# FFN up-projection by seven block products instead of eight, with weight block sums on GpSimd and the residual kept in DRAM

## The chip, the cores and the metric

The kernel runs on one core of a Trainium2 chip. The metric is the device time of one launch in microseconds. Engines are named as the profile names them: PE (TensorE matmul), PEld (TensorE weight load), DVE (VectorE), ACT (ScalarE), POOL (GpSimd), SP (SyncE, which issues most transfers).

## The reference

Two layers of a diffusion backbone over 1280 tokens (256 context, 1024 latent), width 1024, all in fp32. After the token mixers each layer ends with a gated convolution FFN. This is the part that changes:

```
def _conv_ffn(h, w_up, conv_w, conv_b, w_down):
    u = jnp.einsum('bld,df->blf', h, w_up)
    ...
    u = sum(up[:, j:j + l] * conv_w[j] for j in range(CONV_W)) + conv_b
    a, g = jnp.split(u, 2, axis=-1)
    return jnp.einsum('blf,fd->bld', jax.nn.silu(a) * g, w_down)
...
        x = _layer_norm(ALPHA * x + g1_l * jnp.einsum('ble,ed->bld', m_l, w_out[i]), ln1_g[i], ln1_b[i])
        f_l = _conv_ffn(x * (1.0 + sc2_l) + sh2_l, ffn_up[i], ffn_conv_w[i], ffn_conv_b[i], ffn_down[i])
        x = _layer_norm(ALPHA * x + g2_l * f_l, ln2_g[i], ln2_b[i])
```

The hidden width is 2816, so `w_up` has 44 column tiles of 128: 22 value tiles and their 22 gate tiles. The convolution has three taps along the tokens.

## The kernel before

Activations lie transposed: a tile holds 128 features by a run of tokens. The precision of fp32 is had from three reduced-precision products: `split` (lines 211 to 213) writes a rounded high part by ACT (line 212) and the low rest by DVE (line 213), and every matmul is hi·hi + hi·lo + lo·hi. Weights are split as they arrive, activations once per stage.

Per layer the order is: input projection, linear and latent attention, output projection (`wout`), first norm (`ln`), FFN, second norm. The FFN runs over two parts of the tokens: 642 and 638 in layer 0 (context and latent, then latent), 512 and 512 in layer 1. For every one of the 22 hidden tiles `ffn_up` multiplies a value tile and a gate tile: each is 8 K tiles by 3 products by one or two token segments, in `dense` (line 323). ACT copies the result to a tile `u` (line 1141), then comes the convolution (ACT line 1146, DVE lines 1147 and 1148), the SiLU (line 1151), the gate product (line 1152) and the split of the hidden tile. Hidden tiles are multiplied down in groups of four or two (`groups`, line 61): `ffn_down` makes eight output tiles per group (matmuls of line 1180), and DVE adds each to the residual `y` in SBUF by one instruction from PSUM (line 1185).

A few things set the order of the work around it. `ffn_order` (line 43) issues the down product of a group after the first up tile of the next one. `wplan` lists all weights in the order of use, and `wahead` keeps up to four loads and three split weights ahead. Background work (`tick`) emits the norms, the modulation and layer 1's `ada` products a step at a time between the FFN steps. A scheduler then fixes one order for each engine, and every engine runs its list strictly in that order. Tiles of a kind share a fixed number of buffers (`u` 3, `t` 6, `h` 8, `hid` 16, `y` 8, split weights `w2` 7, loads `wst` 4); a new tile waits for the last reader of the one whose buffer it takes. All of PSUM is one tile `ps` of eight banks.

```
    def split(self, hi, lo, src):
        self.nc.scalar.copy(hi, src)
        self.nc.vector.tensor_tensor(lo, src, hi.bitcast(F32), op=ALU.subtract)
```

## Time and profile before

| what | value |
|---|---|
| time, median of 3 runs | 3468.95 us (3467.35 to 3469.02) |
| the profiled execution: span | 3473.9 us, mean granted TensorE clock 0.989 |
| PE busy | 3383.5 us (97%) |
| DVE busy | 2227.2 us (64%) |
| ACT busy | 1548.3 us (45%) |
| POOL busy | 398.5 us (11%) |
| DMA | mean 102 GB/s |

The profile gives one execution; its own time is the span, from the first to the last instruction, 4.95 us above the median of the runs. Busy time is the time in which an engine had at least one instruction in flight, so instructions that overlap count once. The FFN of layer 0 fills 950 to 1900 us of the span, that of layer 1 2705 to 3420 us.

### The profile page before, as it was taken

How to read it: one execution, taken by the hardware profiler on the slowest of the kernel's cores; microseconds unless marked ns; L12 is line 12 of the kernel's file. 1: busy time of each engine (PE TensorE's matmuls, PEld its weight loads, DVE VectorE, ACT ScalarE, POOL GpSimd, SP SyncE). 2: the span in 40 equal slices, each digit the busy share in tenths (PEclk: the TensorE clock that was granted, in tenths of full speed). 3: DMA queues.
4: the chain of work that ended last, by engine and by line, in shares of the span. 5: the costliest groups of instructions: out<-in, count | busy, mean ns of one | idle time of the engine just before them, and what ended most of it. 6: DMA issues, size and time to landing. Idle time of an engine off the chain costs nothing. (4 is left out here: it accounts for less than half of the span.)

```text
span 3473.9 us, 58101 instructions
## 1 busy us (share of the span) xinstructions
PE 3383.5 (97%) x23454; PEld 2919.4 (84%) x23454; DVE 2227.2 (64%) x3787; ACT 1548.3 (45%) x2867; POOL 398.5 (11%) x627
## 2 busy tenths in 40 slices
PE   8999999989999999999999999999999999999998
PEld 6997666768999999899999898766777888888897
DVE  3435878776774444675557734788877765687555
ACT  3334555544453333343334444555563544345433
POOL 0000333331010000000000000333310000001001
PEclk9999999989999999999999999999999999999999
DMA  8654111124223333432223444111124333323331
GB/s 291 203 185 135 29 55 41 40 83 141 74 73 116 122 116 132 147 104 78 75 73 120 161 135 136 36 42 51 38 96 131 96 92 97 97 91 116 98 92 49
DMA packets 174990, 354.95 MB, mean 102 GB/s; under 512 B 15552, under 2 KB 92160, under 8 KB 174720
## 3 DMA queue, kind: packets, MB, share of 16 engines
q1 hardware_dynamic: 174720, 351.23, 31.7%
q8 instruction: 184, 3.01, 0.4%
q14 instruction: 86, 0.70, 0.1%
HBM read 310.01 MB, written 36.44 MB: 100 GB/s over the span
## 5 line engine op out<-in xcount | busy, mean ns | idle before, releaser
L323 PE MATMUL ps<-h,w 128*128 128x320 f32 (+5 forms) x9600 | 1667.4, 334 | 15.1 <-ACT h L212 6.3
L323 PEld LDWEIGHTS ps<-h,w 128*128 128x128 f32 x9600 | 1532.0, 190 | 145.7 <-issue 7.0
L213 DVE TENSOR_TENSOR w<-ws,w 128x1024 fp32r<-128x1024 f32 x360 | 440.1, 1223 | 590.5 <-PE ps L323 294.5
L1180 PE MATMUL ps<-hid,w 128*128 128x256 f32 (+4 forms) x3696 | 576.6, 316 | 1.5 <-ACT hid L212 1.5
L1180 PEld LDWEIGHTS ps<-hid,w 128*128 128x128 f32 x3696 | 538.9, 189 | 36.1 <-issue 7.6
L212 ACT CAST w<-ws 128x1024 fp32r<-128x1024 f32 x360 | 378.8, 1053 | 416.6 <-PE ps L1180 291.2
L919 PE MATMUL ps<-h,h 96*128 96x512 f32 (+1 forms) x1200 | 325.4, 392 | 18.7 <-DVE w L947 14.4
L919 PEld LDWEIGHTS ps<-h,h 96*128 96x128 f32 x1200 | 200.0, 194 | 78.1 <-issue 21.1
L1147 DVE SCALAR_TENSOR_TENSOR t<-u,vec,t 128x642 f32<-128x642 f32 (+3 forms) x176 | 144.6, 821 | 181.9 <-ACT t L1146 181.8
L932 ACT ACTIVATE w<-ps,sm 128x768 f32<-128x768 f32 (+2 forms) x272 | 208.9, 774 | 113.0 <-DVE sm L928 91.2
L1141 ACT COPY u<-ps 128x512 f32<-128x512 f32 (+4 forms) x264 | 118.2, 483 | 310.7 <-PE ps L323 310.7
L1185 DVE SCALAR_TENSOR_TENSOR y<-ps,mod,y 128x320 f32<-128x320 f32 (+5 forms) x376 | 197.0, 557 | 69.0 <-PE ps L1180 68.3
L945 PE MATMUL ps<-ident,w 128*128 128x128 f32 x1312 | 222.3, 287 | 12.1 <-ACT w L932 12.0
L945 PEld LDWEIGHTS ps<-ident,w 128*128 128x128 f32 x1312 | 152.0, 144 | 70.6 <-issue 35.5
L965 POOL TENSOR_SCALAR dg<-ident,sm 128x128 f32<-128x128 f32 x144 | 99.8, 697 | 954.7 <-DVE sm L963 833.4
L1137 POOL MEMSET u<- 128x1 f32 (+1 forms) x264 | 20.9, 102 | 1616.9 <-DVE t L1148 1462.4
L969 PE MATMUL ps<-w,hid 128*64 128x128 f32 x2624 | 196.8, 282 | 3.8 <-DVE y L979 2.0
L969 PEld LDWEIGHTS ps<-w,hid 128*64 128x64 f32 x2624 | 151.8, 139 | 41.2 <-issue 29.1
L921 DVE TENSOR_REDUCE sm<-ps 128x1 f32<-128x1024 f32 x128 | 156.3, 1221 | 43.8 <-PE ps L919 38.8
L949 ACT COPY w<-ps 128x256 f32<-128x256 f32 (+1 forms) x272 | 128.2, 474 | 94.0 <-PE ps L945 92.0
L716 POOL TENSOR_TENSOR hid<-hid,hid 128x512 f32<-128x512 f32 x108 | 146.3, 1371 | 98.5 <-ACT hid L696 69.0
L1146 ACT ACTIVATE t<-u,vec 128x642 f32<-128x642 f32 (+3 forms) x176 | 153.8, 874 | 0.4
(195 smaller groups left out, 3279.4 us busy)
## 6 DMA issues: line engine op xcount, KB each, us to landing
ws<-in_up_dram SPq DMA_DIRECT2D x176, 512.0 KB, 3.6
ws<-in_down_dram SPq DMA_DIRECT2D x88, 512.0 KB, 3.5
ws<-in_ada_dram SPq DMA_DIRECT2D x80, 512.0 KB, 4.8
ws<-in_w_in_dram SPq DMA_DIRECT2D x48, 512.0 KB, 4.3
ws<-in_w_out_dram SPq DMA_DIRECT2D x32, 512.0 KB, 3.7
y<-in_ada_dram SPq DMA_DIRECT2D x16, 512.0 KB, 8.3
ws<-in_w_v_dram SPq DMA_DIRECT2D x16, 512.0 KB, 4.0
hid<-in_xT_dram SPq DMA_DIRECT2D x16, 320.0 KB, 6.1
```

What stands on the lines that cost most here:

```text
L212: self.nc.scalar.copy(hi, src)
L213: self.nc.vector.tensor_tensor(lo, src, hi.bitcast(F32), op=ALU.subtract)
L323: nc.tensor.matmul(ps[:, i, 0:n], w_[:, k, :], h[k][:, part, o:o + n], start=(k == 0 and q == 0), stop=(k == 7 and q == 2))
L716: nc.gpsimd.tensor_tensor(X[n][:], blk(E[n][:, 0, cs[i]]), qx[:], op=ALU.mult)
L919: nc.tensor.matmul(sc[:, o:o + n], q[qa][0:96, qs], K[ka][0:96, o:o + n], start=(x == 0), stop=(x == 2))
L921: nc.vector.tensor_reduce(st[:, 1:2], sc[:, 0:1024], axis=AX.X, op=ALU.max)
L932: nc.scalar.activation(P[:, c0:c1], sc[:, c0:c1], AF.Exp, bias=st[:, 2:3], scale=MSCALE, accum_out=st[:, 3 + j:4 + j])
L945: nc.tensor.transpose(ps[:, t_], P[:, 128 * (t0 + t_):128 * (t0 + t_) + 128], self.ident[:])
L969: nc.tensor.matmul(op[64 * i:64 * i + 64, 0], V[h // 2][t_ // 5][:, t_ % 5, r:r + 64], pts[i][:, t_], start=(t_ == 0), stop=(t_ == nk - 1) ...
L1146: nc.scalar.activation(v[:, 0:n], u[:, 1:1 + n], AF.Identity, scale=cw(j, 1), bias=self.vec[l][:, V_CB + j:V_CB + j + 1])
L1180: nc.tensor.matmul(pb[i][:, 0:n], w[w_][:, x, ms], p.hh[f0 + x][hp][:, o - 1:o - 1 + n], start=(x == 0 and q == 0), stop=(x == gn - 1 and ...
L1185: nc.vector.scalar_tensor_tensor(t, pb[i][:, o:o + n], self.md(l, 5, m, who), t, op0=ALU.mult, op1=ALU.add)
```

## The change

The up product of a pair (value tile A, gate tile G) is written as a 2 by 2 block product. The rows of blocks are the tiles A and G, the inner blocks are the two halves of K (four K tiles each), and the columns are the left and the right half of the part's tokens. Eight half-size products become seven, by the Strassen scheme in Winograd's form:

- For every pair POOL makes four weight sums of 128x512 (`wload`): x0 = G_lo + G_hi, x1 = x0 - A_lo, z0 = A_lo - G_lo, z1 = A_hi - x1. The seven weight blocks (A_lo, A_hi, G_hi and the four sums) are each split by ACT and DVE, as 128x512.
- Once per part `sums` makes the seven activation blocks: DVE forms 16 sums of half the tokens, and 28 half-width blocks are split. It takes the place of `hsplit` (8 full-width splits).
- `ffn_up` issues seven products of 4 K tiles by 3, that is 84 matmuls of 322, 318 or 256 columns, where there were 96 (layer 0: 256 and 386, or 320 and 318 columns) or 48 (layer 1: 512 columns). They go into three banks of a ring of four, in the order 0, 5, 6, 1, 4, 3, 2. In place of ACT's copies, ACT makes two half-width copies (`s1` and one quarter of the result) and DVE five half-width adds from PSUM (`s6`, `s7` and three quarters). Products 1, 4, 3 and 2 accumulate on banks that ACT or DVE has read before.
- The residual is no longer in SBUF during the FFN. The first norm stores its result to a DRAM tile `yd` (SP), the modulation overwrites `y` in place, and of every output tile of the down product ACT scales the PSUM result into a tile `t`, and a transfer that POOL issues adds it to `yd` in DRAM. Before the second norm its tokens are loaded back (SP). The very last group alone still adds by DVE, to rows loaded ahead.
- The groups are one and seven times three hidden tiles for every part. The parts of layer 0 are 644 and 636 tokens. Loads go up to eight list entries ahead, splits up to six buffers.

The diff, cut to its core (the removed comments and unchanged pieces left out):

```diff
-    for n in [2] + [4] * 5 if (l, part) == (NL - 1, 1) else [4] * 4 + [2] * 3:
+    for n in [1] + [3] * 7:
         out.append((f, n))
         f += n
     return out
 
+UNIT = {1: 1024, 3: 256}
...
+PAIR = (0, 5, 6, 1, 4, 3, 2)
...
+PARTS = ((0, 644), (644, T)), ((CTX, 768), (768, T))
...
+        if self.ffn:
+            return self.ps[:, 4:6, :]
...
-                    q += [(a["up"][l, j], [128, 8, 128]) for j in (x, NF + x)]
+                    q += [((l, part, x), i) for i in PAIR]
                 else:
                     f0, gn = groups(l, part)[x]
-                    w, u = a["down"][l, f0:f0 + gn].rearrange("f p o -> p f o"), 1024 // gn
-                    q += [(w[:, :, u * i:u * i + u], [128, gn, u]) for i in range(gn)]
+                    w, u = a["down"][l, f0:f0 + gn].rearrange("f p o -> p f o"), UNIT[gn]
+                    q += [(w[:, :, u * i:u * i + u], [128, gn, u]) for i in range(1024 // u)]
...
+        elif shape == PAIR[0]:
+            l, _, f = src
+            A, G = self.ws([128, 8, 128]), self.ws([128, 8, 128])
+            nc.sync.dma_start(A[:], self.a["up"][l, f])
+            nc.sync.dma_start(G[:], self.a["up"][l, NF + f])
+            x, z = self.yk(shape=(128, 2, 4, 128)), self.yk(shape=(128, 2, 4, 128))
+            lo, hi = slice(0, 4), slice(4, 8)
+            for out, p, q, op in ((x[:, 0], G[:, lo], G[:, hi], ALU.add), (x[:, 1], x[:, 0], A[:, lo], ALU.subtract),
+                                  (z[:, 0], A[:, lo], G[:, lo], ALU.subtract), (z[:, 1], A[:, hi], x[:, 1], ALU.subtract)):
+                nc.gpsimd.tensor_tensor(out, p, q, op=op)
+            self.wsum[src] = {0: (A, A[:, lo]), 1: (A, A[:, hi]), 2: (z, z[:, 1]), 3: (G, G[:, hi]), 4: (x, x[:, 0]), 5: (x, x[:, 1]), 6: (z, z[:, 0])}
...
+        while self.wl < min(self.wi + 8, self.wlim):
+            if self.wsp < self.wl - 3 and isinstance(self.wq[self.wl][0], tuple) and self.wq[self.wl][1] == PAIR[0] and len(self.wsum) > 1:
+                break
+            self.wload(self.wl)
             self.wl += 1
-        while self.wsp < min(self.wi + 3 - len(self.begun), self.wl):
-            shape = self.wq[self.wsp][1]
-            hi, lo = self.w2(shape, F32R), self.w2(shape, F32R)
-            self.split(hi[:], lo[:], self.wst.pop(self.wsp)[:])
-            self.wrd[self.wsp] = (hi, lo)
-            self.wsp += 1
+        n = 2 * len(self.begun)
+        i = self.wi
+        while i < min(self.wl, self.wlim):
+            src, shape = self.wq[i]
+            n += 1 if isinstance(src, tuple) else 2
+            if n > 6:
+                break
+            if i == self.wsp:
+                if isinstance(src, tuple):
+                    t = self.w2([128, 2, 4, 128], F32R)
+                    self.split(t[:, 0], t[:, 1], self.wsum[src].pop(shape)[1])
+                    if not self.wsum[src]:
+                        del self.wsum[src]
+                    self.wrd[i] = (t[:, 0], t[:, 1])
+                else:
+                    hi, lo = self.w2(shape, F32R), self.w2(shape, F32R)
+                    self.split(hi[:], lo[:], self.wst.pop(i)[:])
+                    self.wrd[i] = (hi, lo)
+                self.wsp += 1
+            i += 1
...
+    def ytiles(self, W):
+        t = [self.yk(shape=(128, 2, W)) for _ in range(4)]
+        return [t[k // 2][:, k % 2, :] for k in range(8)]
...
-        Y = [t[:, c0:c1] for t in y]
+        if load is not None:
+            Y = self.ytiles(W)
+            for k in range(8):
+                nc.sync.dma_start(Y[k], load[:, k, c0:c1])
+            yield
...
+    def sums(self, F, W):
+
+        nc, n = self.nc, W // 2
+        left, right = slice(0, n), slice(n, W)
+        X = [[None] * 4 for _ in range(7)]
+        for i in (0, 1):
+            for k in range(4):
+                X[i][k] = self.hid([128, 2, n], F32R)
+                self.split(X[i][k][:, 0], X[i][k][:, 1], F[4 * i + k][:, left])
+        free = []
+        for k in range(4):
+            T_ = {}
+            if k > 1:
+                t = self.yk(F32R, (128, 2, 2, n))
+                T_ = {3: t[:, 0], 2: t[:, 1]}
+            for i in (4, 5, 6) if k > 1 else (4, 5, 3, 6, 2):
+                if not free:
+                    t = self.hs([128, 2, 2, n])
+                    free = [t[:, 0], t[:, 1]]
+                T_[i] = free.pop(0)
+            t, t2 = self.tt([128, 2, n]), self.tt([128, 2, n])
+            z = {4: t[:, 0], 5: t[:, 1], 3: t2[:, 0], 6: t2[:, 1]}
+            b11, b12, b21, b22 = F[k][:, left], F[k][:, right], F[4 + k][:, left], F[4 + k][:, right]
+            nc.vector.tensor_tensor(z[4], b12, b11, op=ALU.subtract)
+            nc.vector.tensor_tensor(z[5], b22, z[4], op=ALU.subtract)
+            nc.vector.tensor_tensor(z[3], b21, z[5], op=ALU.subtract)
+            nc.vector.tensor_tensor(z[6], b22, b12, op=ALU.subtract)
+            for i in (5, 6, 4, 3):
+                self.split(T_[i][:, 0], T_[i][:, 1], z[i])
+            self.split(T_[2][:, 0], T_[2][:, 1], b22)
+            del t, t2, z
+            for i, t in T_.items():
+                X[i][k] = t
+        return X
...
+        def product(i, bank, first):
+            hi, lw = self.wnext()
+            for k in range(4):
+                for q, (w_, part) in enumerate(((hi, 0), (hi, 1), (lw, 0))):
+                    nc.tensor.matmul(bank[:, 0:w], w_[:, k, :], X[i][k][:, part, :], start=(first and k == 0 and q == 0),
+                                     stop=(k == 3 and q == 2), skip_group_check=True)
+        def bank():
+            self.ring = (self.ring + 1) % 4
+            return self.ps[:, self.ring, :]
...
+        st = self.tt([128, 2, w])
+        s1, s6 = st[:, 0], st[:, 1]
+        b1 = bank()
+        product(0, b1, True)
+        nc.scalar.copy(s1, b1[:, 0:w])
+        b2 = bank()
+        product(5, b2, True)
+        nc.vector.tensor_tensor(s6, b2[:, 0:w], s1, op=ALU.add)
+        b3 = bank()
+        product(6, b3, True)
+        s7 = self.tt([128, w])
+        nc.vector.tensor_tensor(s7[:], b3[:, 0:w], s1, op=ALU.add)
+        product(1, b1, False)
+        for c, d, at in pieces(0):
+            nc.scalar.copy(U[0][:, at:at + d - c], b1[:, c:d])
+        product(4, b2, False)
+        plus(U[1], 1, b2, s7)
+        product(3, b3, False)
+        plus(U[1], 0, b3, s6)
+        product(2, b2, False)
+        plus(U[0], 1, b2, s1)
...
-                for i, o, n, cd, who in p.outs:
-                    if i in ss:
-                        t = y[m][:, cd:cd + n]
-                        nc.vector.scalar_tensor_tensor(t, pb[i][:, o:o + n], self.md(l, 5, m, who), t, op0=ALU.mult, op1=ALU.add)
+                if last:
+                    for i, o, n, cd, who in p.outs:
+                        if i in ss:
+                            t = p.Y[m][:, cd - base:cd - base + n]
+                            nc.vector.scalar_tensor_tensor(t, pb[i][:, o:o + n], self.md(l, 5, m, who), t, op0=ALU.mult, op1=ALU.add)
+                else:
+                    t, e = self.tt([128, 644]), 0
+                    for i, o, n, cd, who in p.outs:
+                        nc.scalar.activation(t[:, cd - base:cd - base + n], pb[i][:, o:o + n], AF.Identity, scale=self.md(l, 5, m, who))
+                        e = cd - base + n
+                    nc.gpsimd.dma_start(yd[:, m, base:base + e], t[:, 0:e], accum_op=ALU.add)
...
-        h = net.hsplit(Ff[0], P[0].c1 - P[0].c0)
+        net.ffn = True
+        X = net.sums(Ff[0], P[0].c1 - P[0].c0)
+        Ff[0] = y[0] = None
...
+                    X = net.sums(Ff[1], p.c1 - p.c0)
+                    Ff[1] = y[1] = None
...
+                    else:
+                        d0, d1 = p.done
+                        p.Y = net.ytiles(d1 - d0)
+                        for k in range(8):
+                            nc.sync.dma_start(p.Y[k], yd[:, k, d0:d1])
```

The first place is DVE's list in layer 1's second part, where the group's up tile runs (`w` split weights, `u` the up result, `t` work tiles, `hid` the hidden tile, `hal` the two carried columns). Before, in a row:

```order
L213 TENSOR_TENSOR w_29839<-ws_29798,w_29838 128x1024
L1147 SCALAR_TENSOR_TENSOR t_29832<-u_29828,vec_76,t_29832 128x514
L1148 SCALAR_TENSOR_TENSOR t_29832<-u_29828,vec_76,t_29832 128x514
L1139 COPY u_30180<-hal 128x2
L213 TENSOR_TENSOR w_29883<-ws_29836,w_29882 128x1024
L1147 SCALAR_TENSOR_TENSOR t_29870<-u_29866,vec_76,t_29870 128x514
L1185 SCALAR_TENSOR_TENSOR y_25169<-ps,mod_78,y_25169 128x258
L1148 SCALAR_TENSOR_TENSOR t_29870<-u_29866,vec_76,t_29870 128x514
L1185 SCALAR_TENSOR_TENSOR y_25169<-ps,mod_78,y_25169 128x255
L1152 TENSOR_TENSOR t_29870<-t_29832,t_29870 128x514
```

And now (L256 is the split, L1260 and L1264 are `s6` and `s7`, L1251 the three result quarters, `y` the tiles with the weight sums):

```order
L1260 TENSOR_TENSOR t_31511<-ps,t_31511 128x256
L256 TENSOR_TENSOR w_31574<-ws_31512,w_31573 128x1024
L1264 TENSOR_TENSOR t_31571<-ps,t_31511 128x256
L256 TENSOR_TENSOR w_31590<-ws_31533,w_31590 128x512
L256 TENSOR_TENSOR w_31606<-y_31537,w_31606 128x512
L1251 TENSOR_TENSOR u_31507<-ps,t_31571 128x256
L256 TENSOR_TENSOR w_31622<-y_31538,w_31622 128x512
L1251 TENSOR_TENSOR u_31507<-ps,t_31511 128x256
L256 TENSOR_TENSOR w_31664<-ws_31533,w_31664 128x512
L1282 SCALAR_TENSOR_TENSOR t_31638<-u_31507,vec_76,t_31638 128x514
L1251 TENSOR_TENSOR u_31505<-ps,t_31511 128x256
L1283 SCALAR_TENSOR_TENSOR t_31638<-u_31507,vec_76,t_31638 128x514
```

The adds to the residual are gone, and between the reads of the product banks stand splits of weights for later products.

The second place is POOL's list at a down product of the same part. Before, POOL only clears the edge columns of `u`:

```order
L1137 MEMSET u_30142 128x2
L1137 MEMSET u_30180 128x2
L1137 MEMSET u_30224 128x2
L1137 MEMSET u_30262 128x2
L1137 MEMSET u_30306 128x2
```

Now the weight sums (L218) and the accumulating transfers (L1330, to the DRAM tile) share the list:

```order
L1225 MEMSET u_33235 128x2
L1330 DMA y_26302<-t_32962 128x513
L1330 DMA y_26302<-t_32984 128x513
L218 TENSOR_TENSOR y_33099<-ws_33096 128x512
L1330 DMA y_26302<-t_33012 128x513
L218 TENSOR_TENSOR y_33099<-y_33099,ws_33095 128x512
L218 TENSOR_TENSOR y_33100<-ws_33095,ws_33096 128x512
L218 TENSOR_TENSOR y_33100<-ws_33095,y_33099 128x512
L1330 DMA y_26302<-t_33034 128x513
```

The sums of a coming pair stand behind transfers that wait for ACT's scaled output.

The third place is PE's list where layer 0 goes from its first to its second part. Before, layer 1's `ada` products (L263) stand between the last up tile of one and the first of the other, which walks the K tiles `h` one by one:

```order
L323 MATMUL ps<-h_9261,w_13555 128x386
L263 MATMUL ps<-ws_13748,st 32x256 x4
L263 MATMUL ps<-ws_13754,st 32x256 x4
L323 MATMUL ps<-h_13760,w_13616 128x320
L323 MATMUL ps<-h_13760,w_13616 128x318
```

Now (`h` and `hid` of numbers above 14000 are blocks of the new part, L1318 the down product):

```order
L306 MATMUL ps<-ws_14264,st 32x256 x4
L1242 MATMUL ps<-h_14294,w_14174 128x318 x3
L1242 MATMUL ps<-h_14295,w_14191 128x318 x3
L1242 MATMUL ps<-hid_14270,w_14157 128x318 x3
L1242 MATMUL ps<-hid_14273,w_14157 128x318 x3
L1242 MATMUL ps<-hid_14276,w_14157 128x318 x3
L1242 MATMUL ps<-hid_14279,w_14157 128x318 x3
L1318 MATMUL ps<-hid_13715,w_14429 128x256
L1318 MATMUL ps<-hid_13715,w_14429 128x388
```

The first matmuls of the new part need blocks that `sums` makes on DVE and ACT; six matmuls of the waiting down product stand there before the pair goes on, the other 138 behind it.

## Rows read from the trace of the kernel before

**Rows 1.** The page's part 1, busy time of each engine.
```profile
PE 3383.5 (97%) x23454; PEld 2919.4 (84%) x23454; DVE 2227.2 (64%) x3787; ACT 1548.3 (45%) x2867; POOL 398.5 (11%) x627
```

**Rows 2.** Busy time in windows: layer 0's FFN parts, then layer 1's (columns first).
```profile
core 0: us, PE busy (x) PEld busy (x) DVE busy (x) ACT busy (x) POOL busy (x), PEclk, DMA share, GB/s
950.00:1420.00 470.00, 469.06 (x3321) 450.60 (x3320) 262.73 (x382) 174.49 (x257) 14.54 (x87) 1.00 0.35 115
1420.00:1900.00 480.00, 479.24 (x3285) 474.26 (x3284) 290.93 (x424) 190.48 (x278) 9.15 (x47) 1.00 0.31 95
2705.00:3060.00 355.00, 355.00 (x1533) 287.65 (x1532) 229.29 (x325) 160.06 (x215) 12.72 (x88) 1.00 0.32 94
3060.00:3420.00 360.00, 359.55 (x1968) 310.66 (x1967) 239.51 (x372) 163.53 (x220) 12.18 (x46) 1.00 0.31 97
```

**Rows 3.** The same view, stretches with matmuls of one width: 319, 512, 257.
```profile
1700.00:1800.00 100.00, 100.00 (x683) 100.00 (x682) 50.44 (x71) 32.30 (x46) 0.88 (x8) 1.00 0.26 78
2800.00:2900.00 100.00, 100.00 (x434) 81.20 (x433) 59.27 (x83) 42.95 (x58) 1.78 (x28) 1.00 0.31 95
3230.00:3250.00 20.00, 20.00 (x169) 20.00 (x168) 12.16 (x22) 4.08 (x5) 0.10 (x1) 1.00 0.36 107
```

**Rows 4.** Groups of DVE and ACT: operands, shapes, count | busy us, mean ns | idle before.
```profile
L213 DVE TENSOR_TENSOR w<-ws,w 128x1024 fp32r<-128x1024 f32 x360 | 440.1, 1223 | 590.5 <-PE ps L323 294.5
...
L213 DVE TENSOR_TENSOR h<-hid,h 128x512 fp32r<-128x512 f32 x32 | 20.6, 686 | 0.0
...
L904 DVE TENSOR_TENSOR h<-ps,h 64x256 fp32r<-64x256 f32 x24 | 9.9, 411 | 0.8 <-ACT h L903 0.7
...
L1185 DVE SCALAR_TENSOR_TENSOR y<-ps,mod,y 128x320 f32<-128x320 f32 (+5 forms) x376 | 197.0, 557 | 69.0 <-PE ps L1180 68.3
...
L1147 DVE SCALAR_TENSOR_TENSOR t<-u,vec,t 128x642 f32<-128x642 f32 (+3 forms) x176 | 144.6, 821 | 181.9 <-ACT t L1146 181.8
```

**Rows 5.** DVE's instructions in time during attention: start us, us, instruction.
```profile
358.80 0.76 DVE L693 TENSOR_TENSOR hid<-u 128x512 f32<-128x512 f32 x1
359.49 0.41 DVE L703 TENSOR_TENSOR hid<-hid,u 128x256 f32<-128x256 f32 x1
359.82 0.41 DVE L924 TENSOR_REDUCE sm<-ps 128x1 f32<-128x256 f32 x1
...
360.75 0.90 DVE L703 TENSOR_TENSOR hid<-hid,u 128x256 f32<-128x256 f32 x1
...
362.75 1.50 DVE L765 SCALAR_TENSOR_TENSOR hid<-u 128x256 f32<-128x256 f32 x1
```

**Rows 6.** POOL's instructions in the same stretch.
```profile
360.09 1.28 POOL L716 TENSOR_TENSOR hid<-hid,hid 128x512 f32<-128x512 f32 x1 [1.08 <-ACT hid L696]
361.32 1.23 POOL L712 TENSOR_TENSOR hid<-u,hm 128x512 f32<-128x512 f32 x1
362.63 2.76 POOL L716 TENSOR_TENSOR hid<-hid,hid 128x512 f32<-128x512 f32 x2
```

**Rows 7.** Line L716: duration ns min/median/max, first and last start, form.
```profile
L716 POOL TENSOR_TENSOR hid<-hid,hid x108: 1262/1286/1773, 348.4 to 2505.4; 128x512 f32<-128x512 f32 x108
```

**Rows 8.** DVE's instructions in time at the start of layer 0's FFN.
```profile
935.52 1.23 DVE L213 TENSOR_TENSOR w<-ws,w 128x1024 fp32r<-128x1024 f32 x1 [4.08 <-issue]
936.66 1.00 DVE L1055 SCALAR_TENSOR_TENSOR y<-ps,mod,y 128x320 f32<-128x320 f32 x2
937.58 5.04 DVE L213 TENSOR_TENSOR h<-hid,h 128x642 fp32r<-128x642 f32 x6
...
944.59 1.55 DVE L213 TENSOR_TENSOR h<-hid,h 128x642 fp32r<-128x642 f32 x2
```

**Rows 9.** The page's parts 3 and 6: a DMA queue; two issues, us to landing.
```profile
q1 hardware_dynamic: 174720, 351.23, 31.7%
...
ws<-in_down_dram SPq DMA_DIRECT2D x88, 512.0 KB, 3.5
...
y<-in_ada_dram SPq DMA_DIRECT2D x16, 512.0 KB, 8.3
```

More of the change, by code (lines that the diff above doesn't have):

```diff
@@ L86, in __init__ @@
         self.pairs = 2
+        self.ffn, self.ring = False, 0
         self.begun = []
@@ new lines, in wload @@
+    def wload(self, i):
+        nc, (src, shape) = self.nc, self.wq[i]
+        if not isinstance(src, tuple):
+            t = self.ws(shape)
+            nc.sync.dma_start(t[:], src)
+            self.wst[i] = t
+        elif shape == PAIR[0]:
[9 more added lines that the diff above has]
+            self.wsum[src] = {0: (A, A[:, lo]), 1: (A, A[:, hi]), 2: (z, z[:, 1]), 3: (G, G[:, hi]), 4: (x, x[:, 0]), 5: (x, x[:, 1]), 6: (z, z[:, 0])}
@@ L1102, in ffn_part @@
         p = Bag()
-        c0, c1 = (((0, 642), (642, T)), ((CTX, 768), (768, T)))[l][part]
+        c0, c1 = PARTS[l][part]
         W = c1 - c0
@@ L1117, in ffn_part @@
         else:
-            p.segs = halves(W) if W > 512 else [(0, W)]
-            p.place = [2 + o for o, _ in p.segs]
+            p.segs, p.place = [(0, W)], [2]
             p.npos, p.zero = W + 2, [(W + 2, W + 4)]
@@ L1126, in ffn_part, with ffn_up @@
         return p
-    def ffn_up(self, l, p, f, h):
+    def sums(self, F, W):
[31 more added lines that the diff above has]
+        return X
+    def ffn_up(self, l, p, f, X):
         nc = self.nc
         cw = lambda j, i: self.vec[l][:, V_CW + 3 * j + i:V_CW + 3 * j + i + 1]
-        vs, n = [], p.npos
-        for j in (f, NF + f):
-            ps = self.sc2()
-            self.dense(ps, p.segs, self.wnext(), h)
+        n, W = p.npos, p.c1 - p.c0
+        w = W // 2
+        U = []
+        for _ in range(2):
             u = self.u([128, 646])
@@ L1137, in ffn_up, with pieces, plus @@
                 nc.gpsimd.memset(u[:, z0:z1], 0.0)
+            U.append(u)
+        for u, j in zip(U, (f, NF + f)):
             if p.part:
                 nc.vector.tensor_copy(u[:, 0:2], self.hal[:, j, :])
-            for i, (o, w) in enumerate(p.segs):
-                nc.scalar.copy(u[:, p.place[i]:p.place[i] + w], ps[:, i, 0:w])
+        def pieces(half):
+            for (o, m), at in zip(p.segs, p.place):
+                c, d = max(o, w * half), min(o + m, w * half + w)
+                if c < d:
+                    yield c - w * half, d - w * half, at + c - o
+        def product(i, bank, first):
[7 more added lines that the diff above has]
+            return self.ps[:, self.ring, :]
+        def plus(u, half, b, t):
+            for c, d, at in pieces(half):
+                nc.vector.tensor_tensor(u[:, at:at + d - c], b[:, c:d], t[:, c:d], op=ALU.add)
+        st = self.tt([128, 2, w])
[19 more added lines that the diff above has]
+        plus(U[0], 1, b2, s1)
+        vs = {}
+        for x in (1, 0):
+            u, j = U[x], (f, NF + f)[x]
             if not p.part:
@@ L1189, in ffn_down, with ln_last @@
                 _, _, n, cd, _ = p.outs[ss[0]]
-                yield from self.ln_last(l, cd, cd + n, y)
-    def ln_last(self, l, c0, c1, y):
+                yield from self.ln_last(l, cd, cd + n, [t[:, cd - base:cd - base + n] for t in p.Y])
+    def ln_last(self, l, c0, c1, Y):
         nc = self.nc
         W = c1 - c0
-        Y = [t[:, c0:c1] for t in y]
-        ps, p2 = self.sc2(), self.sc2()
+        ps, p2 = self.ps[:, 0:2, :], self.ps[:, 2:4, :]
         for k in range(8):
@@ L1343 @@
         store = [(net.xs, 0), (out, CTX)][l]
-        ln2 = [net.ln(l, *p.done, y, V_LN2G, V_LN2B, store) for p in P]
+        ln2 = [net.ln(l, *p.done, None, V_LN2G, V_LN2B, store, load=yd) for p in P]
         for op, part, x in ffn_order(l):
@@ L1357 @@
                     net.tick()
-                for _ in net.ffn_down(l, p, x, y):
+                for _ in net.ffn_down(l, p, x, yd):
                     net.tick(1, but=ada)
@@ L1361 @@
                     net.bg.insert(0, ln2[0])
-                if part and x == len(groups(l, part)) - 2 and l == 0:
-                    net.drain(ln2[0])
-                    nx = net.modulate(1, 0, 0, 640, net.loader(net.xs, 0, 640), F)
-                    for _ in nx:
-                        pass
+                if part and x == len(groups(l, part)) - 2:
+                    if l == 0:
+                        net.drain(ln2[0])
+                        nx = net.modulate(1, 0, 0, 640, net.loader(net.xs, 0, 640), F)
+                        for _ in nx:
+                            pass
+                    else:
[3 more added lines that the diff above has]
+                            nc.sync.dma_start(p.Y[k], yd[:, k, d0:d1])
+        del X
+        net.ffn = False
         if l == 0:
```

77 lines of the change are left out of this document (38 added, 39 removed).

## The prediction

> **What bounds the kernel now.** I read the engines' busy time first. PE is busy for 97% of the span, DVE for 64%, ACT for 45%, POOL for 11% [rows 1]. A kernel like that gets shorter by what PE is spared, until another engine's list becomes longer than PE's. So the second view is the windows of the two FFN stretches, the only ones that change [rows 2]. There PE is at 99 to 100% and its clock is granted in full (1.00, so 2.4 GHz). DVE works 553.7 of 950 us in layer 0 (58%) and 468.8 of 715 us in layer 1 (66%), ACT 365.0 and 323.6 us, POOL almost nothing, and the DMA share is about 0.32. The third view, stretches with matmuls of one width, gives PE's price per matmul: 683 in 100 us are 146.4 ns each at about 319 columns, 434 are 230.4 ns at 512, and 169 in 20 us are 118.3 ns at about 257 [rows 3]. A matmul of half the columns therefore costs 0.51 of a whole one. In the last stretch PEld is busy all the time: every narrow matmul has a weight load of its own, and it stays covered.
>
> **What PE is spared.** Layer 0: a pair had 96 matmuls and has 84. 12 x 146.4 ns x 44 pairs are 77 us; the new ones have 322 or 318 columns, a little more than the old mean, which gives back 2: **75 us**. Layer 1: 48 x 230.4 ns = 11.06 us per pair become 84 x 118.3 ns = 9.94 us, 1.12 us x 44 pairs = **49 us**. The eighth product saved is worth half as much there, because halves are dearer per column. Together -124 us: PE's FFN work would be 875 and 666 us. The order of PE's list has exactly 44 x 2 x 84 up matmuls, so the saving itself is certain; the question is what the others need in this time.
>
> **What DVE gets.** Back to back, its instructions start sooner than the one before ends: 0.41 us instructions stand 0.33 us apart [rows 5], so I take 0.08 us off each mean.
> - Weight splits: seven of 512 columns (0.686, so 0.606) for two of 1024 (1.223, so 1.143) [rows 4]: +1.96 us per pair, +86 us per layer.
> - Five adds from PSUM per pair: 0.411 us at 256 columns [rows 4], so 0.33 each, 1.65 per pair in layer 1 (+73 us). For 322 columns I go on along the line through 0.411 (256) and 0.686 (512): 0.48, so 0.40 each (+88 us).
> - The residual adds go: 0.557 [rows 4], so 0.48 us, x 224 in layer 0 (-107 us) and x 136 in layer 1 (-65 us).
> - `sums` adds 16 half-width subtractions and costs 28 half-width splits for 8 whole ones: about +12 us for the second part.
>
> Layer 0: 553.7 + 86 + 88 - 107 + 12 = **633 us**. Layer 1: 468.8 + 86 + 73 - 65 + 10 = **573 us**. Against 875 and 666 both still fit. ACT gets seven half-size copies for two, two narrow copies and the scaling, and loses the whole-width copies; it stays near 60 to 66%, beside PE. The transfers that add to DRAM read and write some 75 MB more, about as many bytes again as a quarter of the traffic now; at 0.32 that is no bound. Reloading the residual and storing it on SP's queue I cost at nothing: each has at least one whole pair (15 us) before its reader, against landings of 3.5 to 8.3 us [rows 9]; without that cover it would be one landing per norm, 8 us.
>
> **What POOL gets, and what it does to DVE.** 176 sums per layer of 128x512. The same form in attention takes 1.286 us [rows 7], so **227 us** per layer; POOL has room. But what POOL does is not free for DVE. In attention [rows 5, 6] a 256-column DVE instruction with both inputs in SBUF that takes 0.41 us alone takes 0.90 when it starts inside a POOL instruction (360.75, under POOL's 360.09 to 361.37), and 1.50 in the next (362.75), while the reduction that reads PSUM is untouched. So POOL's instruction blocks DVE's two-input ones. How much of 227 us falls on DVE is not in this trace; the ends are 0 (POOL runs only beside ACT waits and PSUM reads) and all of it. I take the share of time in which DVE would have such an instruction in hand, since that is what a sum meets. In layer 1, a pair of 15.1 us holds 7 weight splits x 0.606, 4/3 splits for the down product of about 0.87, 4 convolution taps of 0.67 and 2 more of 0.61: 9.3 us, 0.61; with the norms 0.65. In layer 0 the same list over 19.9 us, with the norms, is 0.55.
>
> The Trainium skill, "SBUF — State Buffer", section "Who interferes with whom", states this as a rule: DVE and GpSimd have one pair of ports in common, an instruction holds it whole, and the other fully blocks when a DVE instruction has two SBUF inputs and the GpSimd one reads SBUF. The rows agree with it (0.41 to 0.90 us), and taken at full price for each sum it speaks against this change: it would give the 3529 us of the first rival below instead of my 3440.
>
> DVE then needs 573 + 0.65 x 227 = 721 us in layer 1, against 666 on PE: DVE-bound, so **+55 us**. Layer 0: 633 + 0.55 x 227 = 758 of 875 us (87%). That fits as a sum but not at every moment: product 2 writes the bank that DVE must have read after product 4, with product 3 alone (12 matmuls, 1.8 us) as cover, and between those reads stand weight splits that a sum may block. I charge 0.45 us per pair, **+20 us**, between 0 and 1 us.
>
> **Starts of a part.** At the FFN's start DVE was idle for 4 us and had 8 splits [rows 8]; now it has some 36 half-width instructions more than PE's first product covers: +5 us for each layer, **+10**. At layer 0's second part the first matmuls of the new part stand ahead of most of a down product, and the blocks take buffers that the last products read: **+10 us** (0 to 20). Layer 1's is within DVE's sum already.
>
> Transfers that POOL issues I cannot price from this trace: the ends are 0 and the 8.3 us landing [rows 9] for each. `t` has six buffers, one output comes every 2.1 to 2.65 us (18 matmuls at 118.3 or 146.4 ns), so a landing has 12 us of cover; I take 0.
>
> **Sum.** -124 + 55 + 20 + 10 + 10 = -29 us: span 3473.9 - 29 = 3444.9; the profiled run stands 4.95 us above the median, so **3440 us**.
>
> **Rivals.**
> - *Slower: every sum costs DVE its whole length.* Layer 1: 573 + 227 = 800, +134 over PE. Layer 0: 860 of 875 us, queueing +30. With the starts -124 + 134 + 30 + 20 = +60: **3529 us**. For it: the 1.50 us instruction, which waited for two POOL instructions' worth. Against: PSUM reads pass freely, and they are a third of DVE's list. It decides above a share of 0.78, where 573 + 227 x 0.78 - 666 + 40 eats the 124 us. Chance 0.27.
> - *The covers hold.* The sums fall into DVE's idle time, PE stays the bound in both layers, and only starts and a little queueing remain (28 us): -96, **3373 us**. For it: DVE has 240 and 90 us free before the lock. Against: in layer 1 it takes only a share of 0.41 to use them up. Chance 0.20.
> - *POOL's list holds up the weights.* Sums of a coming pair stand behind transfers that wait for ACT's output, and `t` may be held by a norm. If each of four sums waits for one output (2.65 us) at each of 14 groups in layer 1, and no pair of lead hides it, that is +150 us on top: **3590 us**. Against: loads go eight entries ahead. Chance 0.08.
>
> **Chances.** My forecast has 0.42; its own range is 3390 (a share of 0.5, small starts) to 3475 (0.75). 0.03 is for what I don't see. The 80% range takes in both near rivals: **3365 to 3550 us**. A difference below 0.2% (7 us) a measurement of this kernel can't tell from none. Faster than 3462: all of the second rival and nearly all of the forecast, 0.56. Between 3462 and 3476: its upper edge, 0.07. Slower: the upper end of the forecast's share and the first and last rivals, 0.37.
>
> **What would show it.** If right, the changed kernel's windows show layer 1's FFN near 720 us with DVE above 95% and PE near 92%, and layer 0's near 915 with PE at 95%; weight splits of 512 columns with a mean well above 0.69 us; POOL sums near 1.29 us; PE's waits ending on DVE's reads of `ps` and on `w`. If DVE's splits stay at 0.69 us and PE at 99%, the second rival holds. If layer 1 takes 800 us, the first. If PE waits for weights while DVE itself waits for `y` from POOL, the third. I am wrong altogether if narrow matmuls run slower than 118 ns when their weights come from half-size tiles, or if the granted clock falls below 1.00 in PE's new gaps.

## The result

3758.1 us (median of 4 runs, 3756.6 to 3758.8) against 3469.0 before: a ratio of 1.083, interval 1.0815 to 1.0846. The change is slower by 289 us, where 3440 us and a range of 3365 to 3550 were forecast.

The page's part 1 of the changed kernel, to be held against [rows 1]:

```profile
PE 3381.9 (90%) x24510; PEld 2951.0 (79%) x24510; DVE 2710.2 (72%) x4501; ACT 1909.6 (51%) x3785; POOL 1160.8 (31%) x1227
```

The windows of the two FFNs, from the last matmul of the output projection to the last one of the down product (columns as in [rows 2]):

```profile
960.80:2091.30 1130.50, 965.13 (x6222) 911.39 (x6222) 800.19 (x1143) 573.19 (x1004) 409.82 (x437) 0.92 0.53 132
2867.70:3731.30 863.60, 753.20 (x5322) 704.60 (x5321) 739.26 (x1105) 490.63 (x891) 397.45 (x434) 0.95 0.52 125
```

The same windows of the kernel before:

```profile
942.80:1921.50 978.70, 975.47 (x6776) 950.96 (x6775) 577.08 (x840) 373.81 (x546) 23.69 (x134) 1.00 0.33 105
2700.00:3452.50 752.50, 750.55 (x3737) 631.16 (x3736) 488.88 (x733) 332.79 (x453) 28.38 (x139) 1.00 0.30 91
```

So the two FFNs are longer by 152 and 111 us. Another 18 us lie ahead of FFN0, since layer 0's output projection ends at 942.8 us before and at 960.8 now; the rest is within 2 us. Most of the 18 us are lost in layer 0's input projection: from 50 to 250 us of the span PE is busy for 199.4 us before and 187.6 now. What changed there is `wahead`, which loads up to eight list entries ahead, and PE waits for that layer's own `ada` loads (20 to 300 us, before and now; in total, times, longest):

```profile
PE ps L263 <- DMA ws<-in_ada_dram: 0.5, 1, 0.5
```

```profile
PE ps L306 <- DMA ws<-in_ada_dram: 9.8, 15, 1.7
```

In e4 and e11 below, which have the old `wahead`, that output projection ends at 941.5 and 945.8 us, in all the other experiments between 958 and 966. The look-ahead was not changed by itself.

PE is as busy as before (3382 us), but that says little, for two things are mixed in it. The granted clock has two levels in the records, 2.4 and 1.2 GHz (1.00 and 0.50), and 0.92 and 0.95 are means over both. I summed the granted clock's deficit over the time in which PE was busy: 0 in both FFNs before, 57 and 34 us now. What is left is PE's work at the full clock: 976 -> 909 and 751 -> 720. So of +263 us in the FFNs, PE's work gave -98, idle time +271 and the lowered clock +90. (In what follows "work", "idle" and "clock" are always these three.)

What PE waited for, by the view of waits, in FFN0 and then in FFN1 (us in total, times, longest):

```profile
PE ps L306 <- DMA ws<-in_ada_dram: 66.2, 24, 4.0
PE ps L1318 <- ACT t L1328: 28.4, 17, 6.1
PE ps L1242 <- DVE t L1260: 13.1, 4, 7.2
...
PE ps L1242 <- DVE u L1251: 7.7, 14, 2.0
```

```profile
PE ps L1242 <- DVE u L1251: 29.6, 24, 4.2
PE ps L1318 <- ACT t L1328: 19.1, 11, 5.6
PE ps L1242 <- DVE t L1260: 18.0, 11, 3.2
PE ps L1242 <- DVE t L1264: 12.2, 11, 2.4
```

Three kinds make up most of it: loads of layer 1's `ada` weights (layer 0 only), banks of the down product that ACT has not scaled (L1328), and banks of the seven products that DVE has not read. The groups of DVE and POOL (as in [rows 4]):

```profile
L256 DVE TENSOR_TENSOR w<-y,w 128x512 fp32r<-128x512 f32 x352 | 302.6, 864 | 97.0 <-ACT w L255 95.4 <-PE ps L1242 0.7
L256 DVE TENSOR_TENSOR w<-ws,w 128x512 fp32r<-128x512 f32 x264 | 240.6, 912 | 134.8 <-ACT w L255 133.4
...
L1283 DVE SCALAR_TENSOR_TENSOR t<-u,vec,t 128x514 f32<-128x514 f32 x44 | 39.9, 906 | 0.2
```

```profile
L1330 POOL DMA_DIRECT2D y<-t x248 | 222.2, 1015 | 306.2 <-ACT t L1328 303.8 <-DVE w L256 0.9 <-DVE t L1132 0.9
L218 POOL TENSOR_TENSOR y<-ws,ws 128x512 f32<-128x512 f32 x88 | 148.6, 1688 | 18.4 <-DVE w L256 15.4 <-DVE h L256 2.8
```

The 512-column split takes 0.86 to 0.91 us in place of 0.686, POOL's sums 1.55 to 1.69 in place of 1.286 [rows 7]. The blocking of [rows 5, 6] in the new place, in layer 1's second part (start us, us; the sums are L218, the splits L256):

```profile
3514.49 0.69 DVE L256 TENSOR_TENSOR w<-y,w 128x512 fp32r<-128x512 f32 x1 [0.55 <-ACT w L255]
...
3517.54 1.29 POOL L218 TENSOR_TENSOR y<-y,ws 128x512 f32<-128x512 f32 x1
3517.56 1.82 DVE L256 TENSOR_TENSOR w<-ws,w 128x512 fp32r<-128x512 f32 x1 [2.38 <-ACT w L255]
...
3519.31 2.29 DVE L256 TENSOR_TENSOR w<-y,w 128x512 fp32r<-128x512 f32 x1
3519.45 1.60 POOL L218 TENSOR_TENSOR y<-ws,y 128x512 f32<-128x512 f32 x1
...
3521.52 0.68 DVE L256 TENSOR_TENSOR w<-ws,w 128x512 fp32r<-128x512 f32 x1
```

Two splits that lie beside sums take 1.82 and 2.29 us, those without one 0.69 and 0.68; of the two sums shown, one takes 1.60 us and the other 1.29.

### The profile page after: what moved, and what is told of

Its sections match the earlier page's. It is cut to its first block, busy times and chain, and to the rows that moved or that the text cites. A ratio compares the mean times of both kernels' runs of the same rounds, so it can differ in the third digit from the quotient of the medians.

```text
span 3754.8 us, 63790 instructions
## 1 busy us (share of the span) xinstructions
PE 3381.9 (90%) x24510; PEld 2951.0 (79%) x24510; DVE 2710.2 (72%) x4501; ACT 1909.6 (51%) x3785; POOL 1160.8 (31%) x1227
## 5 line engine op out<-in xcount | busy, mean ns | idle before, releaser
L256 DVE TENSOR_TENSOR w<-ws,w 128x512 fp32r<-128x512 f32 (+2 forms) x476 | 479.1, 1007 | 397.9 <-ACT w L255 137.7
L1242 PE MATMUL ps<-h,w 128*128 128x256 f32 (+2 forms) x4224 | 648.8, 305 | 114.7 <-DVE u L1251 37.3
L1242 PEld LDWEIGHTS ps<-h,w 128*128 128x128 f32 x4224 | 598.4, 195 | 141.4 <-DVE u L1251 44.6
L1318 PE MATMUL ps<-hid,w 128*128 128x256 f32 (+4 forms) x3696 | 615.7, 327 | 60.4 <-ACT t L1328 47.5
L1318 PEld LDWEIGHTS ps<-hid,w 128*128 128x128 f32 x3696 | 567.7, 199 | 98.7 <-ACT t L1328 55.8
L366 PE MATMUL ps<-h,w 128*128 128x320 f32 (+4 forms) x3264 | 549.2, 327 | 11.9 <-ACT h L255 6.3
L366 PEld LDWEIGHTS ps<-h,w 128*128 128x128 f32 x3264 | 509.3, 191 | 52.8 <-issue 15.4
L255 ACT CAST w<-ws 128x512 fp32r<-128x512 f32 (+2 forms) x476 | 361.9, 761 | 259.0 <-PE ps L366 99.8
L256 DVE TENSOR_TENSOR w<-y,w 128x512 fp32r<-128x512 f32 x352 | 302.6, 864 | 97.0 <-ACT w L255 95.4
L1242 PE MATMUL ps<-hid,w 128*128 128x256 f32 (+2 forms) x2112 | 335.3, 308 | 15.8 <-ACT t L1257 9.5
L1242 PEld LDWEIGHTS ps<-hid,w 128*128 128x128 f32 x2112 | 308.6, 199 | 26.8 <-ACT t L1257 11.8
L1330 POOL DMA_DIRECT2D y<-t x248 | 222.2, 1015 | 306.2 <-ACT t L1328 303.8
L255 ACT CAST w<-y 128x512 fp32r<-128x512 f32 x352 | 216.8, 617 | 163.7 <-POOL y L218 72.3
L1328 ACT ACTIVATE t<-ps,mod 128x256 f32<-128x256 f32 (+6 forms) x432 | 211.1, 535 | 113.7 <-PE ps L1318 62.1
L218 POOL TENSOR_TENSOR y<-ws 128x512 f32<-128x512 f32 x88 | 136.4, 1550 | 373.1 <-DMA ws<-in_up_dram 282.9
```

The source lines that it names most:

```text
L218: nc.gpsimd.tensor_tensor(out, p, q, op=op)
L366: nc.tensor.matmul(ps[:, i, 0:n], w_[:, k, :], h[k][:, part, o:o + n], start=(k == 0 and q == 0), stop=(k == 7 and q == 2))
L1242: nc.tensor.matmul(bank[:, 0:w], w_[:, k, :], X[i][k][:, part, :], start=(first and k == 0 and q == 0), stop=(k == 3 and q == 2), skip_gro ...
L1318: nc.tensor.matmul(pb[i][:, 0:n], w[w_][:, x, ms], p.hh[f0 + x][hp][:, o - 1:o - 1 + n], start=(x == 0 and q == 0), stop=(x == gn - 1 and ...
L1328: nc.scalar.activation(t[:, cd - base:cd - base + n], pb[i][:, o:o + n], AF.Identity, scale=self.md(l, 5, m, who))
L1330: nc.gpsimd.dma_start(yd[:, m, base:base + e], t[:, 0:e], accum_op=ALU.add)
```

## The experiments

Unless rounds are named, each is one run beside one run of the kernel before (3468 to 3470 us); e13 and e14 stand beside eight (median 3471 us). The theories, as the expectations name them: A, weights come late, since loads, sums and splits form one chain over four load buffers; B, GpSimd's sums block DVE (the prediction's mechanism, with its size to be tested); C, layer 1's ada products stand in bunches ahead of down products. The prediction's third rival, the transfers, stands beside them. FFN0 and FFN1 are the spans of the two FFNs as above: 978.7 and 752.5 before, 1130.5 and 863.6 with the change. (Where the expectations take 960 or 962 for FFN0 before, they count from 961.7 us, 19 us after the output projection has ended there.)

**e1: ada spread over the up tiles.**

```diff
-                net.tick(2 if ada in net.bg else 1)
+                net.tick(4 if ada in net.bg else 1)
```

> Layer 1's ada products get four background steps per up tile of layer 0 in place of two, so that their eight K tiles no longer stand in a bunch ahead of a down product. Theory C (the bunch: PE waits 66 us for ada loads in the changed kernel, each time behind a load that started only when the one before had been used): layer 0's FFN 1130 -> about 1040 us, total about 3670, the waits of L306 below 15 us. Theory A (late weights: four load buffers for a pair, the next pair and ada): the wait only moves to the weights, total 3730 to 3760. Layer 1's FFN stays at 864 us by both.

Measured: 3755.0 us, FFN0 1133.7, the ada waits 59.5 us in place of 66.2. Theory C falls: with twice as many steps per tile the waits are nearly the same.

**e2: no sums.**

```diff
-            x, z = self.yk(shape=(128, 2, 4, 128)), self.yk(shape=(128, 2, 4, 128))
...
-                nc.gpsimd.tensor_tensor(out, p, q, op=op)
-            self.wsum[src] = {0: (A, A[:, lo]), 1: (A, A[:, hi]), 2: (z, z[:, 1]), 3: (G, G[:, hi]), 4: (x, x[:, 0]), 5: (x, x[:, 1]), 6: (z, z[:, 0])}
+            self.wsum[src] = {0: (A, A[:, lo]), 1: (A, A[:, hi]), 2: (G, G[:, lo]), 3: (G, G[:, hi]), 4: (G, G[:, lo]), 5: (A, A[:, lo]), 6: (G, G[:, lo])}
```

> The four weight sums of a pair are left out; the seven products take raw quarters of A and G (the result is another, the work on PE, ACT, DVE and the transfers the same). Theory B (GpSimd's sums block DVE): DVE's 512-column split falls from 0.85 and 0.91 us to 0.69, DVE's busy time by some 135 us in layer 0 and 165 in layer 1, and layer 1's FFN from 864 to about 720 us, total about 3550. Theory A (late loads, not the lock): DVE's durations fall the same way, but the FFNs stay above 1050 and 820 us, total above 3650.

Measured: 3581.3 us; FFN0 1066.7, FFN1 748.7, DVE busy 678 and 591 us (from 800 and 739). The sums cost 177 us, DVE gives back 122 and 148. Layer 1 is then level with the kernel before; layer 0 is still 88 us above it.

**e3: no adding transfers.**

```diff
-                    nc.gpsimd.dma_start(yd[:, m, base:base + e], t[:, 0:e], accum_op=ALU.add)
```

> The transfers that add the down product to the residual in DRAM are left out (the FFN's output is missing from the sum); ACT still scales into t. The prediction's third rival (POOL's list and t's buffers hold things up): the FFNs fall by 60 us each or more, total below 3640. Theories A to C: below 30 us in all, total 3725 to 3760.

Measured: 3670.9 us; FFN0 1099.8, FFN1 811.4. So the transfers that I priced at nothing cost 87 us, more than theories A to C allowed and somewhat less than the rival asked.

**e4 and e11: eight products again, with and without the transfers.** The old `ffn_up` (with its PSUM banks), `wahead` and `hsplit` in place of the new ones; groups, scaling, `yd` and the parts as in the change. e11 also has e3's edit.

```diff
-                    q += [((l, part, x), i) for i in PAIR]
+                    q += [(a["up"][l, j], [128, 8, 128]) for j in (x, NF + x)]
...
-        X = net.sums(Ff[0], P[0].c1 - P[0].c0)
+        X = net.hsplit(Ff[0], P[0].c1 - P[0].c0)
```

> The seven products are undone (eight products, whole tiles, weights split as 1024 columns, no sums), and the rest of the change is kept: groups of three, scaling by ACT, accumulating transfers, residual reloaded. If all the loss is in the seven products: FFNs 960 and 753 us as before, total about 3470. Theory C (ada's bunches come from groups of three, whatever the product): layer 0's FFN 30 to 70 us above 962, total 3500 to 3545. If the transfers hold things up: layer 1's FFN above 775.

> Eight products as before, and the adding transfers left out: against 3503 us with them. If they are the 33 us that the run with eight products lies above the kernel before: 3465 to 3475. If it is the groups of three or ada: 3490 to 3505.

Measured: 3502.6 and 3490.1 us. The residual's new path costs 33 us by itself, 12 of them the transfers, 21 the rest (groups of three, scaling on ACT, storing and reloading), which I have not taken apart. The seven products, with the look-ahead that came with them, cost the other 255. The total of e4 lies at the edge of theory C's range, but PE's wait for layer 1's ada loads is 3.4 us with the same groups: theory C falls again. FFN0 is 997.3 us there, 19 above the kernel before, and FFN1 761.0.

**e5, e10, e7: the sums' blocking alone.** In e5 POOL makes the sums as in the change, and the products read raw quarters as in e2; e10 is e5, and e7 is e2, without the transfers (e3's edit).

The edit of e5 is that of e2 to the line `self.wsum[src]` alone.

> GpSimd makes the four weight sums of every pair as in the change, but nothing reads them: the products take raw quarters of A and G, as in the run without sums (3581 us). So the blocking of DVE stays and the wait of the splits for the sums goes. If the 177 us that leaving the sums out gave were the blocking alone (the prediction's mechanism): 3730 to 3760 us. If they were the wait for late sums alone: 3580 to 3600. Blocked DVE durations stay at 0.85 to 0.91 us for a 512-column split in either case.

> GpSimd makes the sums, nothing reads them, and there are no adding transfers behind them in its list: what is left of the sums is the blocking of DVE alone. Against 3534 us without either. If the blocking alone makes the sums' cost: 3660 to 3690 (as the run with sums in use and without transfers, 3671). If most of it was GpSimd's list, sums that wait for loads with transfers behind them: 3540 to 3590.

> Both the sums and the adding transfers are left out (3581 without the sums alone, 3671 without the transfers alone). If the 87 us of the transfers come from sums that stand behind them in GpSimd's list, nothing is left of them without sums: 3570 to 3585. If they come from the six t buffers that the transfers hold, they are had again: 3490 to 3520.

With e2, e3, e6 and e13 they fill a table (us):

| sums | with transfers | without | the transfers cost |
|---|---|---|---|
| on POOL, used | 3758 | 3671 | 87 |
| on POOL, not used | 3778 | 3664 | 114 |
| on DVE | 3664 | 3599 | 65 |
| none | 3581 | 3534 | 48 |

e10 lies in the range for blocking alone, e5 18 us above its own, and e7 between its two expectations. Down the third column: sums that nobody reads cost 130 us, used ones 137. So it is not that splits wait for sums (theory A's chain): POOL's running itself is the cost. The sums also read the load buffers and write to `y`, but of waits on a sum the view of their line has only 13.8 us in e10, ACT's in four places. The windows of e7 and then of e10, FFN0 and FFN1 (columns as above):

```profile
966.00:2005.80 1039.80, 934.47 (x6223) 891.27 (x6222) 676.48 (x1144) 572.72 (x1002) 28.10 (x134) 0.94 0.32 106
2778.80:3510.70 731.90, 714.87 (x5322) 681.46 (x5321) 590.61 (x1107) 493.60 (x891) 25.20 (x138) 0.98 0.31 104
```

```profile
964.50:2055.20 1090.70, 951.68 (x6222) 902.25 (x6221) 791.80 (x1144) 572.10 (x1003) 313.03 (x310) 0.93 0.30 101
2827.20:3640.00 812.80, 738.77 (x5321) 694.59 (x5321) 737.02 (x1107) 488.44 (x891) 310.46 (x313) 0.96 0.28 94
```

The same 1144 and 1107 DVE instructions are busy for 115 and 146 us more with POOL's sums beside them. The group that shows it in e7, without sums, next to the 864 and 912 ns above:

```profile
L252 DVE TENSOR_TENSOR w<-ws,w 128x512 fp32r<-128x512 f32 x616 | 420.7, 690 | 282.0 <-ACT w L251 277.2
```

**e6 and e13: sums on DVE,** with and without the transfers.

```diff
-                nc.gpsimd.tensor_tensor(out, p, q, op=op)
+                nc.vector.tensor_tensor(out, p, q, op=op)
```

> The four sums of a pair move from GpSimd to DVE: no blocking, and DVE gets 4 x 0.61 us x 44 pairs = 107 us more per layer. If blocking costs DVE more than its own work would (135 and 165 us measured in the changed kernel), layer 1's DVE time falls from 739 to about 700 and its FFN from 864 to about 800, total 3640 to 3700. If DVE's strict order makes every sum wait for a load with all other DVE work behind it, the FFNs get longer instead: above 3760.

> Sums on DVE (3664 us with the adding transfers) and the transfers left out. The transfers cost 87 us beside GpSimd's sums and 48 without sums. If the other 39 come from one GpSimd list that holds both: 48 us here, 3610 to 3622. If they come from DVE being fuller with the sums, on whichever engine: 75 to 90 us here, 3574 to 3590.

Measured: 3664.1 us, within the first range; FFN1 808.4, DVE 689 us there. DVE does all the sums itself in less time than POOL's sums cost it. With the transfers away, 3599.0. Their price, 65 us, lies between the two expectations: of the 39 us that come only when sums and transfers meet, 17 remain with the sums on DVE, so about that much belongs to DVE's fuller list and the other 22 to POOL's one list. One run each; I leave it at "both".

**e8: ada's sections 2 to 5 moved into layer 1's projection.**

```diff
-            ada = net.after(net.ada(1, [(None, s) for s in range(6)]))
+            ada = net.after(net.ada(1, [(None, s) for s in range(2)]))
...
             h = net.hsplit(F, 640)
+            ada = net.after(net.ada(1, [(None, s) for s in (2, 3, 4, 5)]))
```

> Two thirds of layer 1's ada products (sections 2 to 5) are made during layer 1's projection, as layer 0 does with its own, in place of layer 0's FFN. If the ada loads wait for the four load buffers that a pair and the next hold in the FFN: FFN0 1130 -> about 1045 (22 us of work moved, some 45 us of waits and their clock gone), the middle stage 776 -> about 800, total about 3690 to 3705. If the wait passes to the weights: total 3740 to 3760.

Measured: 3754.4 us. FFN0 fell to 1051.0, as expected, but the stage between the FFNs rose from 776 to 852: there too PE waits 38.9 us for ada loads. The work was moved and the wait with it, into that stage and not, as the second expectation has it, to the weights.

**e9 and e14: ada in buffers of its own.** e7 (no sums, no transfers) with one more edit; e14 is the same kernel in 3 rounds.

```diff
-            ada = net.after(net.ada(1, [(None, s) for s in range(6)]))
+            ada = net.after(net.ada(1, [(None, s) for s in range(6)], alloc=lambda s: net.yk(shape=s)))
```

> As the run without sums and without adding transfers (3534 us), and layer 1's ada tiles take buffers of y, which are free there, in place of the four load buffers. If the 68 us for which PE waits for ada loads come from the load buffers that a pair holds until its last splits: FFN0 1040 -> about 950 us, waits of ada's matmuls below 10 us, total 3435 to 3455, below the kernel before. If those transfers are only slow beside the other traffic: FFN0 above 1010, total above 3505.

> The run with sums and adding transfers left out and ada in buffers of its own once more, timed in rounds (3453 us in the single run). It says what seven products for eight could give if sums and transfers were free: 3450 to 3456 us, a ratio to the kernel before of 0.994 to 0.997.

Measured: 3453.3 us, FFN0 1039.8 -> 963.6. In rounds 3454.7 us against 3471.5, ratio 0.9958, interval 0.9944 to 0.9972. The windows of e9:

```profile
960.30:1923.90 963.60, 920.61 (x6222) 883.91 (x6222) 676.02 (x1144) 572.95 (x1002) 29.19 (x134) 0.98 0.34 114
2698.20:3428.50 730.30, 713.29 (x5321) 679.95 (x5320) 590.52 (x1107) 494.10 (x891) 25.22 (x137) 0.98 0.31 104
```

The wait of ada's matmuls in e9 (L302 there), next to 66.2 us above:

```profile
PE ps L302 <- DMA y<-in_ada_dram: 7.9, 6, 1.8
```

So the loads were not slow; they had no buffer, and the part of theory A that names the four load buffers holds for `ada`. The timeline of the changed kernel at one of its ada bunches:

```profile
1227.27 14.24 SPq L301 DMA_DIRECT2D ws<-in_ada_dram  x4
...
1235.46 0.76 PE L306 MATMUL ps<-ws,st 128*32 128x256 f32 x8 [2.64 <-DMA ws<-in_ada_dram]
...
1240.04 1.08 PE L306 MATMUL ps<-ws,st 128*32 128x256 f32 x8 [3.82 <-DMA ws<-in_ada_dram]
...
1244.72 1.08 PE L306 MATMUL ps<-ws,st 128*32 128x256 f32 x8 [3.60 <-DMA ws<-in_ada_dram]
```

Four loads pass one after another, the matmuls of each 4.6 us behind those of the one before. PE's gaps there are followed by the lower clock: eight matmuls take 1.08 us in place of 0.76, and the stretch reads

```profile
1235.90:1249.60 13.70, 5.80 (x35) 3.63 (x32) 1.58 (x5) 2.42 (x5) 0.88 (x1) 0.50 0.44 120
```

By the program, a weight tile gave its `wst` buffer back after one split before. Now a pair's A and G keep theirs until the fourth and the sixth of seven splits (in e7 and e9 the fourth and the seventh), and POOL's sums read them too. So two of four buffers are held for most of a pair, the coming pair and the down weights want the others, and the background loads go through what is left one by one. No view counts buffers; that they were what was missing is shown by e9.

**e12: scaled outputs in `y`.** e2 with another buffer.

```diff
-                    t, e = self.tt([128, 644]), 0
+                    t, e = self.yk(shape=(128, 644)), 0
```

> As the run without sums (3581 us), and ACT's scaled outputs lie in buffers of y, which are free there, so that the six t tiles are left to the convolution and the norms. If the 48 us that the transfers cost without sums come from t buffers that wait for a landing: 3535 to 3550. If they come from the traffic beside the weights' loads: 3570 to 3585.

Measured: 3630.7 us, 49 above e2, so neither expectation. I had miscounted: a norm's reload leaves `y` only two buffers, fewer than the six of `t` were. Read as it is, it says that the buffers do matter. PE's wait for the scaling in FFN0, first in e12, then in e2:

```profile
PE ps L1314 <- ACT y L1324: 25.7, 21, 8.1
```

```profile
PE ps L1314 <- ACT t L1324: 12.1, 8, 3.5
```

An output holds its buffer until POOL has issued the transfer and it has landed, 5.4 to 7.4 us by the medians on the changed kernel's page. Whether six buffers alone make the 48 us that the transfers cost without sums, or the traffic beside the loads too, stays open; more `t` buffers were not tried. Both have a sign in the traces: a load for the up product lands after 4.2 us in e2 and after 3.3 in e7 (medians of the pages), and in e2 ACT's scaling waits 21.5 us for a transfer to give its `t` back.

## Why the prediction was wrong

The forecast was 3440 us and the time 3758. That POOL blocks DVE was right, and by how much; what failed is the step from DVE's busy time to time, the transfers at 0, the load buffers and the clock.

**PE's saving: right.** -124 us forecast. With everything else out of the way (e9), PE's work is 903 and 704 us against 976 and 751: -72 and -47, where I had -75 and -49. The starts of the parts (+20) were not tried by themselves; in e9 PE is idle for 4.3 us of the first 40 in FFN0, 3.8 in FFN1 and 9.0 of the 40 around the start of FFN0's second part, in the change for 10.1, 12.0 and 13.5.

**DVE's busy time and the blocking: right.** The 633 and 573 us forecast without blocking stand for windows of 950 and 715 us [rows 2], 29 and 37 us short of the FFNs. What they add to the kernel before is 79 and 104 us; e7 has 676 and 591 us against 577 and 489, so 99 and 102 more. The blocked shares were 0.55 and 0.65 of 227 us, so 125 and 148; in the changed kernel against e2 they are 122 and 148. The rule that I weighed (the Trainium skill, "SBUF — State Buffer", "Who interferes with whom") holds in e5 and e10 without any data between the two engines. The first rival, full price, doesn't hold: it needed a share above 0.78, and 122 and 148 us are 0.54 and 0.65.

**From DVE's sum to time: wrong.** This is the step "DVE needs 721 us in layer 1, against 666 on PE: DVE-bound, so +55 us", with +20 for queueing in layer 0. It supposes that an engine with a strict order can be filled to the last microsecond. In e10, where only sums that nobody reads were added to e7, FFN1 is 813 us with DVE busy for 737, 91%, and PE idle for 74. DVE's splits wait for ACT's copies (134.8 us of idle time before one group of L256 in the change, above), and behind them in its list stand the reads for which PE waits (in e10, from 2800 to 3550 us, 17.7 us for L1251's and 16.2 for L1260's). The blocking cost 81 us in layer 1 and 51 in layer 0 (e10 against e7), not 55 and 20. So the sign "DVE above 95%" in layer 1's FFN did not come either: in the change it was 86%.

**The transfers, "I take 0": wrong.** 87 us in the change, 48 without sums. The 12 us of cover for a landing were counted as if all six `t` tiles were the outputs', and the convolution, the block sums and the norms hold some; how much of the 48 us that explains is open (e12). The third rival had the right place for a part of the rest (sums and transfers in one list) and too high a price: together they add 39 us, some 22 of them by the one list, not 150.

**Load buffers: not in the sum at all.** I charged the change to engines and queues and never asked how long a pair holds its two `wst` buffers. Price, without sums and transfers: 3534 - 3453 = 80 us, 62 of them idle time of PE and 17 its clock, both in FFN0. The 18 us ahead of FFN0 come with the look-ahead and were not in the sum either: I took the two FFNs to be "the only ones that change".

**The clock: named as a danger, not priced.** At 1.00 before; 0.92 and 0.95 now: 90 us over both FFNs. It goes with PE's idle time there: 5 us of idle and none of clock before, 60 and 27 in e9, 276 and 90 in the change. Every idle microsecond in FFN0 came with 0.3 of clock (57 to 165 us).

Taken along one path, from e9 to the change: -16 us of gain with the sums and transfers left out, +80 for ada's buffers, +48 for the transfers, +177 for the sums (their meeting with the transfers within it): 3758. e9 also answers the second rival, "the covers hold", 3373 us: even there PE's idle time and clock (60 and 27 us, from 5 and 0) take back 82 of the 119 us, and the stretch ahead of FFN0 another 18.

No run here beats the kernel before with the whole computation. e14 has two parts of it left out and is 0.4% (17 us) faster. Its FFN0 still starts 15 us later than before, as it does (by 15 to 23) in every run with the new look-ahead. My estimate from these two numbers is that this form of seven products could give about 1% here at most; no run shows it without that delay.

## What to carry to other kernels

When one engine is spared by giving work to others, the summed busy time of the fullest engine is only a lower bound: with strict orders and covers of one product, FFN1 of e10 came out at 1.10 times DVE's busy time, with DVE at 91%. Count buffers as one counts instructions: of every tile that is now held longer, ask how long, who else draws from the same few, and put the background work among them. And before asking what a fast matrix scheme costs, take its new work out and time the rest; here that ceiling was 17 us. And compare the stages that should not change as well: here one of them lost 18 us.

## What the runs showed of the hardware

The blocking goes both ways, so a GpSimd sum costs twice: DVE's share, and its own, from a median of 1.286 us [rows 7] to means of 1.55 to 1.69 by the groups. It also reaches instructions with a single input. DVE's copy of two edge columns takes 0.36 us in the change and 0.17 in e7 with POOL quiet:

```profile
L1229 DVE COPY u<-hal 128x2 f32<-128x2 f32 x88 | 31.2, 361 | 0.8
```

```profile
L1225 DVE COPY u<-hal 128x2 f32<-128x2 f32 x88 | 14.3, 167 | 0.8
```

The Trainium skill, "SBUF — State Buffer", "Who interferes with whom", counts `copy` among the operations that can take the shared ports in a faster mode. The two rows agree with it. The rows of DVE's reads of PSUM stay where they were (0.415 us at 256 columns in the change, 0.411 in [rows 4]), as forecast.
